# Layer 0 of a two-layer encoder: transposed inputs with the norm's factor applied behind the products, and the first output projection begun beside the last attention group

## The chip, the cores and the metric

The kernel runs on one core of one Trainium2 chip. The metric is the device time of one execution in microseconds (us). The kernel before was run three times: 2688.71, 2690.17 and 2694.2 us, median 2690.17 us.

Five engines work side by side, each with its own queue of instructions that it runs strictly in order: TensorE (PE, products into PSUM banks), VectorE (DVE), ScalarE (ACT), GpSimd (POOL), and SyncE (SP), which issues most DMA transfers. An instruction that waits holds up everything behind it on its engine. A PSUM bank holds 128x512 float32 numbers; there are eight.

## The reference, cut to what matters

```
h = x                                        # 1024 tokens, 1024 channels
mem_n = rmsnorm(mem, mem_norm_g)             # 256 memory tokens
for layer in range(2):
    u = rmsnorm(h, norm_g[layer, 0])
    mem_kv = mem_n @ w_mem_kv[layer]
    if layer == 0: y = mixer_window_attn(u, mem_kv, ...)   # this change is here
    else:          y = mixer_hgrn2(u, mem_kv, ...)
    h = h + rmsnorm(y, norm_g[layer, 1])
    h = h + rmsnorm(conv_ffn(rmsnorm(h, norm_g[layer, 2]), ...), norm_g[layer, 3])

rmsnorm(x, g) = x * rsqrt(mean(x*x, axis=-1) + 1e-6) * g
mixer_window_attn: q, k, v, xq = split(u @ w_in); rotary on q and k;
    16 heads of 64 over a band of 384 keys, 4 cross heads of 128 over mem_kv;
    y = concat(attention (1024 wide), cross (512 wide)) @ w_out
```

The factor `rsqrt(mean + 1e-6)` is one number for each token. It can be multiplied in before a product over the channels, or behind it.

## The kernel before, in words

Every float32 product is made of three products of a faster format: each operand is cut into a high and a low part (`split`: ACT rounds the high part, DVE subtracts for the low part), and `mm3` issues high x high, high x low and low x high. The normed input stands transposed in `uh` and `ul` (high and low; eight blocks of 128 channels by 1024 tokens). Weights come as units of 128x1024: `wunit` loads one into a staging buffer `st` (four of them), and cuts it into `wh`, `wl`, a ring of four.

**Start (`start`, `memory_kv`).** Rows of 128 tokens are loaded; `norm_T` (lines 105 to 121) squares and sums them on ACT (L100), raises the mean to the power -0.5 on POOL (L93, one number for each partition), multiplies on DVE (L112), turns them by eight transposes on PE (L116) and splits the result: first two tiles of memory rows into `mh`, `ml`, then eight tiles of `x` into `uh`, `ul`. `memory_kv` multiplies the memory by the key and value weights of both layers. For each of four heads it makes a 128x256 result of 24 matmuls in one of four banks `pb`, and ACT copies it out (L159), which frees the bank; then four units fill two banks of values at once, 48 matmuls of 512 columns, copied out at L172. Each unit is followed by a `step()`, which norms and turns one tile of `x`.

**Layer 0 (`window`).** `proj(g)` projects a group of four heads into two banks `pj`, multiplies by `cos` and `sin` (L274, L275), adds on POOL (L276, L277) and transposes into the bank `ptq`; `attend(g)` makes scores (L315, L316), softmax, transposes (L338) and `po` (L341, L342), and writes `o` to the HBM tensor `oT`. Cross-attention heads (`cross_unit`) stand between. Groups 0 to 2 alternate with projections; group 3 comes last, when `psq` (the three banks `pj`, `pj`, `ptq`) has been released.

**First output projection (`WOut`).** It has 12 blocks of 128 channels: 0 to 5 (heads of groups 0 to 2), 8 to 11 (cross heads), 6 and 7 (group 3). `open(3, 2)` takes the three released banks and, for five of the eight token tiles, multiplies the blocks 0 to 5 and 8 to 11 for the first half of the output columns beside `attend(3)`. Each call of `products` reads its blocks back from `oT` by a DMA (L436) and splits them again. `finish` adds the blocks 6 and 7, does the other three tiles, then the second half of the columns, and the norm. The class `Out`, which is in the kernel already, does the same for layer 1: it keeps blocks 0 to 7 in `uh`, `ul` themselves and multiplies from there:

```
def read(self, ks, c0, c1, eng):
    c = (slice(None), slice(ks[0], ks[-1] + 1), slice(c0, c1))
    raw = ul[c].bitcast(F32)
    eng.dma_start(raw, oT[self.l][ks[0]:ks[-1] + 1, :, c0:c1].rearrange("k p t -> p k t"))
    act.copy(uh[c], raw)
    dve.tensor_tensor(ul[c], raw, uh[c].bitcast(F32), op=ALU.subtract)
def begin(self, psb, tags, y0):       # for each tile t: read blocks 0 to 5, then
        ps = self.bank()
        self.kept(ps, t, self.groups[0], True, True)
        act.copy(y0[t], ps)
```

The order on each engine is not that of the code: a scheduler in the compiler sets it. `tc.high_priority` moves an instruction ahead of others that are ready.

Of the kernel before, what the change touches and what calls it, by code (L numbers as in the profile page):

```python
# [30 lines left out]
MEM_POOL = 1  # L31
# [15 lines left out]
def build(tc, A, out):  # L47
# [15 lines left out]
    nc.sync.dma_start(ident, A["ident"])  # L63
# [84 lines left out]
    def memory_kv(tp, psb, mh, ml, step):  # L148

        for l in range(2):  # L150
            km = tp.tile([P, 4, 256], F32, tag="km", bufs=1, name="km")
            vm = tp.tile([P, 2, 512], F32, tag="vm", bufs=1, name="vm")
            for h in range(4):
                wh, wl = wunit(A["wmk"][l, h], eng=pool if 4 * l + h < MEM_POOL else None)
                ps = psb.tile([P, 512], F32, tag="pb", name="pb")
                for k in range(KT):
                    c = slice(k * P, (k + 1) * P)
                    mm3(ps[:, :256], wh[:, c], wl[:, c], mh[:, k, :], ml[:, k, :], k == 0, k == KT - 1)
                act.copy(km[:, h, :], ps[:, :256])  # L159
                step()  # L160
# [10 lines left out]
            for t in range(2):  # L171
                act.copy(vm[:, t, :], pv[t])  # L172
# [12 lines left out]
    def cross_unit(l, h, b, head, wp, tags, w0, pair):  # L185
# [12 lines left out]
        for i in range(2):  # L198
# [6 lines left out]
            dve.tensor_scalar_mul(st["nm"][:, e], st["nm"][:, e], -XSCALE)  # L205
            for j in range(2):
                q = 2 * i + j
                act.activation(p[:, q, :], s[:, j, :], AF.Exp, bias=st["nm"][:, q:q + 1],
                               scale=XSCALE, accum_out=st["su"][:, q:q + 1])
# [17 lines left out]
    def window():  # L227
# [7 lines left out]
        nc.sync.dma_start(sin, A["sin"])  # L235
        wmask = ap_.tile([P, 384], F32, bufs=1, name="wmask")
# [15 lines left out]
        def proj(g):  # L252
# [6 lines left out]
            for b in range(2):  # L259
                rqs = []  # L260
                for tt in range(4):
# [17 lines left out]
                    act.copy(v[:, t, :64], ps[:, 320:])  # L279
                    dve.tensor_tensor(v[:, t, 64:], ps[:, 320:], v[:, t, :64].bitcast(F32), op=ALU.subtract)  # L280
# [19 lines left out]
        def attend(g, qkv):  # L300
            qs, kh, kl, v = qkv
            for b in range(2):
                for nn in range(4):
# [42 lines left out]
                    if nn % 2 == 1:  # L346
# [24 lines left out]
    class WOut:  # L371

        groups = (range(0, 6), range(8, 12), range(6, 8))

        def __init__(self, l, src, key, order):
            self.l, self.src, self.key, self.order = l, src, key, order
            self.pools = [[], [], []]
            self.pre, self.part, self.begun, self.us = {}, {}, {}, {}
            self.psb, self.tag, self.psb2 = None, "pb", None

        def open(self, npre, nsb):

            l = self.l
            self.w1 = tc.alloc_tile_pool(name=f"wa{l}", bufs=2, reuse_waits="tile")
            if self.psb is None:
                self.psb = tc.alloc_tile_pool(name=f"wopb{l}", bufs=npre, space=PSUM, reuse_waits="tile")
            self.pools = [[self.w1] for _ in range(3)]
            if l == 0:

                self.w1.tile([P, 512], F32, tag="part", bufs=nsb, name="part")  # L390
                for g in (0, 2):
                    self.operands(g)
                for _ in range(2):
                    for x in ("xwh", "xwl"):
                        self.w1.tile([P, 1024], F32R, tag=x, name=x)
                self.operands(1)
            self.load(0)
            for t in self.order[npre:npre + nsb]:
                ps = self.bank()
                self.products(ps, t, 0)  # L400
                self.products(ps, t, 1, True)
                self.part[t] = self.w1.tile([P, 512], F32, tag="part", bufs=nsb, name="part")
                act.copy(self.part[t], ps)
            for t in self.order[:npre]:
                self.pre[t] = self.bank()
                for g in range(2):
                    self.products(self.pre[t], t, g)

        def bank(self):
            if self.psb2:  # L410
                return self.psb2.tile([P, 512], F32, tag="pb2", name="pb")
            return self.psb.tile([P, 512], F32, tag=self.tag, name="pb")

        def load(self, b, n=6):
            for i, u in enumerate((0, 1, 2, 4, 5, 3)[:n]):
                if (b, u) not in self.us:
                    self.us[b, u] = wunit(A[self.key][b, u], pl=self.w1 if i >= RING else None)
            self.b = b

        def products(self, ps, t, g, last=False, first=False, left=False):  # L420

            ks = [k for k in self.groups[g] if not (left and k in self.begun[t])]
            n = len(ks)
            oh, ol, raw = (x[:, :n, :] for x in self.operands(g))
            self.rows_of(ps, t, ks, oh, ol, raw, g == 0 or first, g == 2 or last)

        def operands(self, g):
            pl = self.pools[g][0]
            self.pools[g] = self.pools[g][1:] + self.pools[g][:1]
            m = len(self.groups[g])  # L430
            return [pl.tile([P, m, P], dt, tag=f"{x}{g}", bufs=1, name=x) for x, dt in (("oh", F32R), ("ol", F32R), ("or", F32))]

        def rows_of(self, ps, t, ks, oh, ol, raw, first, last):
            n = len(ks)
            ts_ = slice(t * P, (t + 1) * P)
            self.read = nc.sync.dma_start(raw, oT[self.l][ks[0]:ks[0] + n, :, ts_].rearrange("k p t -> p k t"))  # L436
            split(oh, ol, raw)
            for i, k in enumerate(ks):
                wh, wl = self.us[self.b, k // 2]
                c = slice((k % 2) * 512, (k % 2 + 1) * 512)  # L440
                mm3(ps, oh[:, i, :], ol[:, i, :], wh[:, c], wl[:, c], first and i == 0, last and i == n - 1)

        def rows(self, wp, t):
            x = wp.tile([P, D], F32, tag="x", bufs=2, name="x")
            nc.sync.dma_start(x, self.src[t * P:(t + 1) * P, :])
            return x

        def finish(self):
            l = self.l
            self.wf = tc.alloc_tile_pool(name=f"wf{l}", bufs=1, side="right", reuse_waits="tile") if l == 0 else None  # L450
            wp = tc.alloc_tile_pool(name=f"wo{l}", bufs=2, side="right", reuse_waits="tile")
            psp = tc.alloc_tile_pool(name=f"wops{l}", bufs=2, space=PSUM, side="right", reuse_waits="tile")
            w2 = tc.alloc_tile_pool(name=f"wb{l}", bufs=2, reuse_waits="tile")
            self.psb2 = tc.alloc_tile_pool(name=f"wopc{l}", bufs=(3, 4)[l], space=PSUM, reuse_waits="tile")
            self.pools[0].append(w2)
            y0 = wp.tile([P, NT, 512], F32, bufs=1, name="y0")
            s0 = wp.tile([P, NT], F32, bufs=1, name="s0")
            for t in self.order:
                ps = self.pre.get(t) or self.bank()
# [40 lines left out]
            w2.release()  # L500
            self.w1.release()

# [978 lines left out]
```

## Time and profile before

| | |
|---|---|
| median of 3 runs | 2690.17 us |
| profiled execution, its own time | 2686.47 us |
| its span | 2684.7 us |
| mean granted TensorE clock | 0.993 |
| PE busy, share of span | 98% |
| first product on the memory | 13.99 us |
| first product of layer 0 (`pj`) | 67.77 us |
| first product of the feed-forward part | after 594.38 us |

Times in the profile count from the start of the span. A timeline row gives the start, the duration, the engine, the line, the operation, `out<-in`, the shape and, in brackets, how long the engine had been idle and what ended that. Durations of matmuls overlap: the rate is read from the starts of rows that follow each other. In a table by stretches the first number behind the stretch is its length, then the busy time of each engine, then the granted clock of PE, the share of the DMA engines and GB/s.

### The profile page before, as it was taken

What the parts mean: (1) busy time and instruction counts of PE and PEld (TensorE: products, weight loads), DVE (VectorE), ACT (ScalarE), POOL (GpSimd) and SP (SyncE); (2) the same over time, 40 slices, a digit from 0 to 9 for tenths busy, and PEclk for the clock granted to TensorE, in tenths of its full rate; (3) what the DMA queues carried; (4) which work ended last, traced back from release to release, by engine and by line L of the source; (5) the groups of instructions that cost most, each with busy time, mean ns of one, the idle gap of its engine ahead of it and who ended that gap; (6) DMA issues with size and microseconds to landing.
All of it is one profiled execution on the core that took longest, in us unless ns stands there. A gap on an engine that the chain in (4) does not pass through costs nothing.

```text
span 2684.7 us, 39333 instructions
## 1 busy us (share of the span) xinstructions
PE 2618.3 (98%) x14496; PEld 2200.0 (82%) x14496; DVE 1827.6 (68%) x3026; ACT 1384.6 (52%) x2530; POOL 469.4 (17%) x520
## 2 busy tenths in 40 slices
PE   8999999999999999999999999999999999999998
PEld 7888897788888887887888888888888788888886
DVE  6587787678656565478778686796757755656456
ACT  6367666645444445455455454545534444444453
POOL 1231110111111100032223132230211111110013
PEclk9999998999999999999999999999999999999999
DMA  7674213557877756674326252102436777774666
GB/s 281 213 166 104 60 28 117 176 183 181 216 199 200 205 165 243 191 241 157 103 84 177 76 120 70 48 29 83 150 119 178 183 202 210 198 205 160 220 196 228
DMA packets 204626, 427.00 MB, mean 159 GB/s; under 512 B 20112, under 2 KB 66576, under 8 KB 198800
## 3 DMA queue, kind: packets, MB, share of 16 engines
q1 hardware_dynamic: 171168, 326.68, 37.5%
q0 software_dynamic: 24544, 90.19, 16.1%
q10 hardware_dynamic: 8720, 7.60, 0.9%
q8 instruction: 114, 1.87, 0.3%
q14 instruction: 80, 0.66, 0.1%
HBM read 331.08 MB, written 117.44 MB: 167 GB/s over the span
## 4 chain that ended last, share of the span: by engine, by line
PE 77%; DVE 13%; ACT 4%; DMA 3%; issue 2%; POOL 1%; SPq 0%; DVEq 0%; ACTq 0%; POOLq 0%
PE X L638 27%; PE V L638 11%; PE pj L81 5%; PE pj L82 5%; PE Y L638 5%; PE pj L83 5%; PE pb L82 3%; PE pb L81 3%; PE pb L83 3%; DVE E L1194 1%; DVE ER L1229 1%; PE pt L338 1%; PE pt L116 1%; DVE wl L87 1%; PE po L1297 1%
## 5 line engine op out<-in xcount | busy, mean ns | idle before, releaser
L87 DVE TENSOR_TENSOR wl<-st,wh 128x1024 fp32r<-128x1024 f32 (+1 forms) x238 | 263.5, 1114 | 325.7 <-ACT wh L86 318.3
L86 ACT CAST wh<-st 128x1024 fp32r<-128x1024 f32 (+1 forms) x238 | 222.5, 937 | 295.2 <-PE X L638 196.2
L81 PE MATMUL pj<-uh,wh 128*128 128x512 f32 x512 | 204.1, 399 | 3.8 <-DVE xl L87 2.5
L638 PE MATMUL X<-wl,wh 128*128 128x512 f32 x528 | 204.8, 390 | 0.3 <-DVE wl L87 0.3
L638 PE MATMUL X<-wh,wl 128*128 128x512 f32 x528 | 204.6, 389 | 0.0
L82 PE MATMUL pj<-ul,wh 128*128 128x512 f32 x512 | 202.5, 396 | 0.1
L83 PE MATMUL pj<-uh,wl 128*128 128x512 f32 x512 | 201.6, 394 | 0.0
L638 PE MATMUL X<-wh 128*128 128x512 f32 x528 | 198.8, 390 | 1.7 <-DVE c L1014 0.9
L81 PE MATMUL pj<-wh,uh 128*128 128x384 f32 (+1 forms) x512 | 190.4, 372 | 4.2 <-DVE gs L1125 3.8
L82 PE MATMUL pj<-wl,uh 128*128 128x384 f32 (+1 forms) x512 | 187.3, 366 | 0.0
L83 PE MATMUL pj<-wh,ul 128*128 128x384 f32 (+1 forms) x512 | 186.8, 366 | 0.0
L77 DVE TENSOR_TENSOR wl<-st,wh 128x1024 fp32r<-128x1024 f32 (+1 forms) x92 | 119.9, 1310 | 28.1 <-ACT wh L76 27.4
L638 PE MATMUL V<-uh,wh 128*128 128x512 f32 x344 | 133.8, 389 | 0.0
L638 PE MATMUL V<-ul,wh 128*128 128x512 f32 x344 | 133.8, 389 | 0.0
L638 PE MATMUL V<-uh,wl 128*128 128x512 f32 x344 | 133.8, 389 | 0.0
L76 ACT CAST wh<-st 128x1024 fp32r<-128x1024 f32 (+1 forms) x99 | 99.9, 1015 | 50.5 <-PE pj L82 27.8
L638 PEld LDWEIGHTS X<-wh 128*128 128x128 f32 x528 | 99.1, 188 | 22.9 <-issue 1.3
L81 PEld LDWEIGHTS pj<-uh,wh 128*128 128x128 f32 x512 | 96.7, 189 | 24.2 <-DVE xl L87 2.9
L638 PEld LDWEIGHTS X<-wl,wh 128*128 128x128 f32 x528 | 99.1, 188 | 21.2 <-DVE wl L87 0.7
L638 PEld LDWEIGHTS X<-wh,wl 128*128 128x128 f32 x528 | 99.1, 188 | 20.8
L83 PEld LDWEIGHTS pj<-uh,wl 128*128 128x128 f32 x512 | 96.8, 189 | 19.2
L980 POOL TENSOR_TENSOR c<-c,g 128x512 f32<-128x512 f32 x24 | 43.4, 1828 | 393.8 <-PE X L638 162.8
(372 smaller groups left out, 7257.4 us busy)
## 6 DMA issues: line engine op xcount, KB each, us to landing
st<-hid SPq DMA_DIRECT2D x154, 256.0 KB, 3.1
st<-in_ffw_dram SPq DMA_DIRECT2D x108, 256.0 KB, 3.2
w2s<-in_ffw_dram POOLq DMA_DIRECT2D x24, 1024.0 KB, 7.9
st<-in_ffw_dram SPq DMA_DIRECT2D x46, 512.0 KB, 4.1
hid<-tt SPq DMA_DIRECT2D x88, 256.0 KB, 4.6
st<-w2s SPq DMA_DIRECT2D x88, 256.0 KB, 2.8
sx<-in_ffw_dram SPq DMA_DIRECT2D x84, 256.0 KB, 3.9
sy<-in_ffw_dram SPq DMA_DIRECT2D x42, 512.0 KB, 6.2
```

What stands on the lines that cost most here:

```text
L76: act.copy(h[:, :n], raw)
L77: (eng or dve).tensor_tensor(l[:, :n], raw, h[:, :n].bitcast(F32), op=ALU.subtract)
L81: pe.matmul(o, ah, bh, start=first, stop=False)
L82: pe.matmul(o, ah, bl, start=False, stop=False)
L83: pe.matmul(o, al, bh, start=False, stop=last)
L86: act.copy(h, src)
L87: dve.tensor_tensor(l, src, h.bitcast(F32), op=ALU.subtract)
L116: pe.transpose(ps[:, k, :], u[:, (4 * b + k) * P:(4 * b + k + 1) * P], ident)
L338: pe.transpose(tp[:, j, :], sm[:, j, c * P:(c + 1) * P], ident)
L638: pe.matmul(o, x, y, start=new, stop=e, skip_group_check=not first)
L980: pool.tensor_tensor(y[q][:, t, :], y[q][:, t, :], g3[:, c], op=ALU.mult)
L1194: dve.tensor_tensor_scan(B[:, rev], smask, a_[:, rev], 0.0, op0=ALU.mult, op1=ALU.add)
```

## The change

The host gives `x` and `mem` transposed as well (`xT`, `memT`) and the two gains as columns (`gT`). `start` no longer norms rows: it loads 128 channels at a time, and `scaled` makes the high and low parts of `x * g` directly (ACT, then DVE). The norm's factor is made apart. For the memory, ACT squares all of it, POOL folds eight blocks into one, PE sums over partitions by a product with ones (`pbc`, a copy of the 256 sums in every partition, and `pcc`), DVE adds epsilon, and POOL raises a whole 128x256 tile to the power -0.5 (`rsb`) and a 128x2 one (`rsm`). The keys are multiplied by `rsb` when they leave their banks (DVE; it was a copy on ACT), the values by `rsm`. For `x` the squares are added up on POOL in `acc`, and eight small products, one POOL power over 128x8 (`rs0`) and two DVE multiplications (`xsc`) follow `memory_kv`. `cos` and `sin` are multiplied by `rs0`, so are the values `v`, and the cross scores of layer 0 use `xsc` in place of a constant. The first memory unit is split on DVE like the others, no longer on POOL (`MEM_POOL` goes). No transposes are left in `start`: 80 matmuls of 128x128 are gone.

Layer 0's output projection uses `Out`. `psq` isn't released: `begin` multiplies blocks 0 to 5 of all eight tiles into its three banks and copies the results to `y0`. Group 3 writes `o` straight into blocks 6 and 7 of `ul` by DMA, not to `oT`.

```
-                wh, wl = wunit(A["wmk"][l, h], eng=pool if 4 * l + h < MEM_POOL else None)
+                wh, wl = wunit(A["wmk"][l, h])
...
-                act.copy(km[:, h, :], ps[:, :256])
+                if l == h == 0:
+                    begin()
+                dve.tensor_tensor(km[:, h, :], ps[:, :256], rsb, op=ALU.mult)
...
-                act.copy(vm[:, t, :], pv[t])
+                act.activation(vm[:, t, :], pv[t], AF.Copy, scale=rsm[:, t:t + 1])
...
+        dve.tensor_tensor(cos, cos, bc(rs0.unsqueeze(2), [P, NT, 32]), op=ALU.mult)
+        s2 = sin.rearrange("p t a b -> p t (a b)")
+        dve.tensor_tensor(s2, s2, bc(rs0.unsqueeze(2), [P, NT, 64]), op=ALU.mult)
...
-                    if nn % 2 == 1:
+                    if nn % 2 == 1 and g == 3:
+                        ts_ = slice((n - 1) * P, (n + 1) * P)
+                        oh, ol = uh[:, 6:8, ts_], ul[:, 6:8, ts_]
+                        for hp in range(2):
+                            nc.sync.dma_start(ul[hp * 64:(hp + 1) * 64, 6:8, ts_].bitcast(F32), o[:, hp::2, :])
+                        act.copy(oh, ol.bitcast(F32))
+                        dve.tensor_tensor(ol, ol.bitcast(F32), oh.bitcast(F32), op=ALU.subtract)
...
-        psq.release()
         ea.release()
         attend(3, cur)
-        wo0.open(3, 2)
+        wo0.open()
+        y0 = wo0.w1.tile([P, NT, 512], F32, bufs=1, name="y0")
+        wo0.begin(psq, ("pj", "pj", "ptq"), [y0[:, t, :] for t in range(NT)])
...
-            for t in self.order:
+            for i, t in enumerate(self.order):
+                if i == (6, 0)[l]:
+                    self.banks += late
+                    self.used = (3, 0)[l]
...
+        def scaled(h, l, raw, g):
+            act.activation(h, raw, AF.Identity, scale=g)
+            dve.scalar_tensor_tensor(l, raw, g, h.bitcast(F32), op0=ALU.mult, op1=ALU.subtract)
...
+        def memory_rstd():
+            for k in (0, 4):
+                act.activation(msq[:, k:k + 4], mT[:, k:k + 4], AF.Square)
+            for n in (4, 2, 1):
+                pool.tensor_tensor(msq[:, :n], msq[:, :n], msq[:, n:2 * n], op=ALU.add)
+            pb = pss.tile([P, 256], F32, name="pbc")
+            pe.matmul(pb, ones, msq[:, 0], start=True, stop=True)
+            ms = tp.tile([P, 256], F32, name="mms")
+            dve.tensor_scalar(ms, pb, 1.0 / D, EPS, op0=ALU.mult, op1=ALU.add)
+            with tc.high_priority(AHEAD):
+                pool.tensor_tensor(rsb, ms, bc(nhalf[:, 0:1], [P, 256]), op=ALU.pow)
...
+        left = [None, None] + list(range(KT))
...
+            raw = tp.tile([P, T], F32, tag="x", bufs=4, name="x")
+            nc.sync.dma_start(raw, A["xT"][k])
+            scaled(uh[:, k], ul[:, k], raw, gT[:, 1, k:k + 1])
...
+                sq = tp.tile([P, T], F32, tag="sq", bufs=2, name="sq")
+                act.activation(sq, raw, AF.Square)
+                pool.tensor_tensor(acc, acc, sq, op=ALU.add)
...
-    wo0 = WOut(0, A["x"], "wout0", list(range(NT)))
+    wo0 = Out(0, A["x"], "wout0", list(range(NT)))
```

What the scheduler makes of it is seen at three places. The first is POOL's queue at the start. Before, it holds the ten norm factors of one column each (`nrs`) and one split:

```order
L65 MEMSET nhalf 128x8
L93 ISA
L93 TENSOR_TENSOR nrs<-nms,nhalf 128x1 x2
L77 TENSOR_TENSOR wl<-st,wh 128x1024
L93 TENSOR_TENSOR nrs<-nms,nhalf 128x1 x8
```

Now it holds the folding of the memory's squares, two additions of `x` squares, the power over 256 columns (`rsb`), and the other additions behind it:

```order
L1277 TENSOR_TENSOR msq<-msq 128x1024
L1277 TENSOR_TENSOR msq<-msq 128x512
L1277 TENSOR_TENSOR msq<-msq 128x256
L1306 TENSOR_TENSOR acc<-acc,sq 128x1024 x2
L1283 TENSOR_TENSOR rsb<-mms,nhalf 128x256
L1289 TENSOR_TENSOR rsm<-mm_174,nhalf 128x2
L1306 TENSOR_TENSOR acc<-acc,sq 128x1024 x5
```

One power of 256 columns has taken the place of ten of one column.

The second is PE between the last key head and the first value unit of the first layer. Before, the products go on from heads to values with nothing between:

```order
L81 MATMUL pb<-mh,wh 128x256
L82 MATMUL pb<-ml,wh 128x256
L83 MATMUL pb<-mh,wl 128x256
L81 MATMUL pb<-wh,mh 128x512 x2
L82 MATMUL pb<-wl,mh 128x512
```

Now the sums over partitions stand inside the last head:

```order
L1279 MATMUL pbc<-msq,ones 128x256
L1286 MATMUL pcc<-ones,msq 128x1 x2
L80 MATMUL pb<-ml,wh 128x256
L81 MATMUL pb<-mh,wl 128x256
L79 MATMUL pb<-mh,wh 128x256
L80 MATMUL pb<-ml,wh 128x256
L81 MATMUL pb<-mh,wl 128x256
L79 MATMUL pb<-wh,mh 128x512
```

The 128x512 row is the first value product. It goes into the bank of head 0, and now waits for the DVE multiplication that reads `rsb` and empties that bank.

The third is PE at the beginning of `attend(3)` (`ps` are its scores, `pt` its transposes, `pb` the output projection). Before, the scores of four blocks of queries and the first `po` come before the first output product:

```order
L315 MATMUL ps<-kh,qs 128x384 x2
L342 MATMUL po<-pl,v 128x512
L338 MATMUL pt<-ident,sm 128x128 x4
L316 MATMUL ps<-kl,qs 128x384 x2
L81 MATMUL pb<-wh,oh 128x512
L82 MATMUL pb<-wl,oh 128x512
```

Now output products, 18 in a row for each tile, begin behind the first scores:

```order
L79 MATMUL po<-ph,kvh 128x512
L322 MATMUL ps<-kh,qs 128x256
L323 MATMUL ps<-kl,qs 128x256
L79 MATMUL pb<-wh,uh 128x512
L80 MATMUL pb<-wl,uh 128x512
L81 MATMUL pb<-wh,ul 128x512
```

The first two tiles' products, 36 matmuls, have moved ahead of nearly all scores of group 3.

More of the change, by code (lines that the diff above doesn't have):

```diff
@@ L29 @@
 STAGE = 4
-MEM_POOL = 1
 QKV_POOL = (0, 2, 2, 2)
@@ new lines, in start @@
+        mh = tp.tile([P, KT, 256], F32R, name="mh")
+        ml = tp.tile([P, KT, 256], F32R, name="ml")
+        for k in range(0, KT, 2):
+            act.dma_start(mT[:, k:k + 2], A["memT"][:, k:k + 2])
+        def scaled(h, l, raw, g):
+            act.activation(h, raw, AF.Identity, scale=g)
+            dve.scalar_tensor_tensor(l, raw, g, h.bitcast(F32), op0=ALU.mult, op1=ALU.subtract)
+        for k in range(KT):
+            scaled(mh[:, k], ml[:, k], mT[:, k], gT[:, 0, k:k + 1])
+        msq = tp.tile([P, KT, 256], F32, name="msq")
@@ new lines, in start @@
+        memory_kv(tp, psb, mh, ml, rsb, rsm, memory_rstd, step)
+        nc.sync.dma_start(ident, A["ident"])
+        pt = pss.tile([P, NT], F32, name="ptt")
+        for t in range(NT):
+            pe.matmul(pt[:, t:t + 1], acc[:, t * P:(t + 1) * P], ones[:, 0:1], start=True, stop=True)
+        ms = tp.tile([P, NT], F32, name="xms")
+        dve.tensor_scalar(ms, pt, 1.0 / D, EPS, op0=ALU.mult, op1=ALU.add)
+        pool.tensor_tensor(rs0, ms, nhalf, op=ALU.pow)
+        dve.tensor_scalar_mul(xsc[:, 0], rs0, XSCALE)
```

189 lines of the change are left out of this document (43 added, 146 removed).

## Prediction

> **What bounds the kernel now.** I read the page's first part, then tables by stretches for the two stages that the change touches, then their timeline rows.
>
> ```profile
> PE 2618.3 (98%) x14496; PEld 2200.0 (82%) x14496; DVE 1827.6 (68%) x3026; ACT 1384.6 (52%) x2530; POOL 469.4 (17%) x520
> ```
>
> PE is busy nearly always, so a change pays where PE idles, runs at a lower clock, or does work that can go. The table of the start and of the stretch from the last projection to the feed-forward part:
>
> ```profile
> 13.99:67.77 53.78, 53.63 (x354) 49.20 (x353) 42.26 (x51) 37.50 (x60) 6.20 (x8) 1.00 0.78 273
> 403.98:594.38 190.40, 180.17 (x839) 147.02 (x838) 136.11 (x278) 116.72 (x253) 21.18 (x24) 0.96 0.52 160
> 400.00:430.00 30.00, 24.80 (x99) 18.43 (x98) 27.13 (x69) 24.23 (x56) 4.10 (x4) 0.72 0.48 141
> 430.00:480.00 50.00, 50.00 (x254) 42.27 (x253) 33.40 (x90) 31.50 (x78) 0.00 (x0) 1.00 0.35 98
> 480.00:500.00 20.00, 15.96 (x79) 12.40 (x79) 11.18 (x21) 11.58 (x25) 0.00 (x0) 1.00 0.33 85
> ```
>
> At the start PE works without a pause from its first product on the memory (13.99 us) to the first product of layer 0 (67.77). POOL does 6 us in that time. The output stage loses 190.4 - 180.2 = 10.2 us to idle PE and 4% of the clock, 7.2 us: 17.4 us in all. Of it, 5.2 us idle and 28% of 30 us, 8.4, lie at 400 to 430, before the output products have begun, and 4.0 at 480 to 500, at the tail of `attend(3)`.
>
> The rates of PE come from starts of neighbouring rows: 0.21 us for a 256-column product just after PE has begun, 0.12 later, 0.227 for 512 columns, 0.17 for the 384 of a projection; four transposes take 0.44 us in the chain of waits.
>
> ```profile
> 15.10 0.41 PE L83 MATMUL pb<-mh,wl 128*128 128x256 f32 x1
> 15.31 0.41 PE L81 MATMUL pb<-mh,wh 128*128 128x256 f32 x1
> ...
> 21.15 0.28 PE L82 MATMUL pb<-ml,wh 128*128 128x256 f32 x1
> 21.27 0.28 PE L83 MATMUL pb<-mh,wl 128*128 128x256 f32 x1
> ...
> 61.65 0.39 PE L82 MATMUL pb<-wl,mh 128*128 128x512 f32 x1
> 61.87 0.39 PE L83 MATMUL pb<-wh,ml 128*128 128x512 f32 x1
> ...
> 67.77 0.33 PE L81 MATMUL pj<-wh,uh 128*128 128x384 f32 x1
> 67.94 0.34 PE L82 MATMUL pj<-wl,uh 128*128 128x384 f32 x1
> ```
> ```profile
> 17.80 0.44 PE pt L116 x4
> ```
>
> **The power over 256 columns.** The price that decides is one which the trace does not hold at this size. It holds the same POOL operation at one and at four columns (min/median/max in ns):
>
> ```profile
> L93 POOL TENSOR_TENSOR nrs<-nms,nhalf x34: 538/548/3790, 6.6 to 2043.7; 128x1 f32<-128x1 f32 x34
> L93 POOL TENSOR_TENSOR ors<-oms,nhalf x16: 1006/1036/1146, 1374.0 to 1937.9; 128x4 f32<-128x4 f32 x16
> ```
>
> Three more columns cost 488 ns, 0.163 us each. By that line 256 columns take 0.548 + 255 x 0.163 = 42.1 us (40.3 by the minima). The lower bound is POOL's additions:
>
> ```profile
> 80.08 0.86 POOL L276 TENSOR_TENSOR rq<-t,t 128x320 f32<-128x320 f32 x1 [0.30 <-DVE t L275]
> 80.92 0.31 POOL L277 TENSOR_TENSOR rq<-t,t 128x64 f32<-128x64 f32 x1
> ```
>
> 256 more columns cost 0.55 us there, 0.0021 us each, so at that rate the power takes 0.55 + 0.55 = 1.1 us. I take 42, because the rows of the power itself are nearer than those of another operation, and nothing in them shows columns that come for nothing.
>
> The Trainium skill, page "GPSIMD Engine Reference", section "3.1 Elementwise — side-by-side cycle accounting", counts about 2.6 cycles an element for a two-input elementwise instruction, some 2.2 ns at the page's 1.2 GHz. The additions agree with it; the power's 0.163 us a column does not, being 75 times that. An estimate by that page would be near 1 us, and the change then ends as in the first rival.
>
> **Who waits for it.** PE's order puts the first value product into the bank of head 0. Four banks hold the four heads, so PE can do 96 products (11.5 us warm) and must then wait until DVE has multiplied head 0 by `rsb`. DVE has put its multiplications behind all eight `ul` splits, which need no `rsb`.
>
> **When the power starts.** ACT has 21 instructions ahead of the square that POOL's second `acc` addition needs, and does that square too. The nearest rows:
>
> ```profile
> 1.18 0.42 SPq L1376 DMA_DIRECT2D x<-in_mem_dram  x1
> 5.08 1.06 ACT L100 ACTIVATE nu<-x 128x1024 f32<-128x1024 f32 x1 [3.06 <-DMA x<-in_mem_dram]
> 10.12 1.05 ACT L76 CAST wh<-st 128x1024 fp32r<-128x1024 f32 x1
> 11.24 2.53 POOL L77 TENSOR_TENSOR wl<-st,wh 128x1024 fp32r<-128x1024 f32 x1 [1.01 <-ACT wh L76]
> 19.71 0.38 ACT L159 COPY km<-pb 128x256 f32<-128x256 f32 x1
> ```
>
> Eight scalings of 128x256 at 0.38, two squares of 1024 columns at 1.06, four weight casts at 1.05, three scalings and three squares of `x` at 1.06: 3.0 + 2.1 + 4.2 + 6.4 = 15.7 us. The first 512 KB landed at 5.08; the first 256 KB of `memT` will be a little earlier, 4.5. So the square is done at 20.2. The two additions at 2.53 run from 18.1, when the first one's square is there, to about 23.2. `pbc` does not come later: the memory's squares end near 13, folding takes 2.5 + 1.3 + 0.7. I put the power at 23.5 to 65.6 us (by a slower DMA, 26).
>
> **The start, summed.** DVE's multiplication and two handovers take 0.7 us: PE resumes at 66.3. What is left for it: 48 x 0.227 + 96 x 0.12 + 48 x 0.227 = 33.3 us, the eleven small products at a transpose's 0.11 about 1, and a slow beginning as at 14 us, 16 products at 0.09 us extra, 1.5. `pj` begins at 102.1 in place of 67.77: **+34.3 us**. The removed transposes, 80 x 0.11 = 8.8 us, and PE's first product some 8 us earlier all lie before the end of the power and gain nothing. Queued behind the power on POOL are `rsm` (0.7) and five additions (12.7): three squares on ACT wait for those because `sq` has two buffers, and the next weight cast stands behind them, 10 us after the power; PE reaches it after 0.7 + 10.9 + 1.5, so it comes in time. SP's loads fill the four staging buffers meanwhile.
>
> **The beginning of layer 0.** Before, PE idles 2.1 + 0.45 us there, since `cos`, `sin` and the sink arrive late:
>
> ```profile
> 78.39 0.33 PE L286 MATMUL ptq<-ident,rq 128*128 128x128 f32 x1 [2.12 <-POOL rq L276]
> 79.17 0.66 PE L81 MATMUL pj<-wh,uh 128*128 128x384 f32 x1 [0.45 <-DVE v L280]
> ```
> ```profile
> 76.46 0.49 DVE L274 TENSOR_TENSOR t<-pj,cos 128x320 f32<-128x320 f32 x1
> ```
>
> They still come from the same place in SP's queue. DVE now has two more multiplications between their arrival and the first `t`, of 256 and 512 columns; at 0.49 for 320 they take 0.4 + 0.7: **+1.1 us**. The 128x8 power, 0.55 + 7 x 0.163 = 1.7 us, lies beside two tiles of projection (48 x 0.17 = 8.2 us). The scaled forms for `v` and the cross scores replace instructions of the same size, one for one: nothing.
>
> **The output stage.** All 576 products stay. Before, the first came at 426.95:
>
> ```profile
> 426.95 0.39 PE L81 MATMUL pb<-wh,oh 128*128 128x512 f32 x1
> ...
> 594.38 1.06 PE L116 MATMUL pt<-ident,nu 128*128 128x128 f32 x8 [0.99 <-DVE nu L112]
> ```
>
> Now 36 of them, 36 x 0.227 = 8.2 us, stand among the scores where 13.6 us were lost, and products of the second half of the columns stand ahead of the last `po`, where 4.0 us were idle. I take 8.2 + 4.0: **-12.2 us**. The bounds are -17.4, the whole loss, and 0: DVE is busy 27.1 of 30 us at 400 to 430, and if the scores wait for it just as long, the moved products only leave their old place empty. A new wait is possible: the `ul` reads of eight tiles stand in SP's queue between the writes of `o`, and PE waits for their splits with scores behind. They are issued while `proj(3)` still runs, so I charge nothing.
>
> **Sum.** 34.3 + 1.1 - 12.2 = +23.2 us. Against the profiled execution (2686.47, its span 2684.7 and 1.8 around it) 2709.7; the median of the runs shown is 3.7 above that execution, so I predict **2713 us**, 0.9% slower.
>
> **Rivals.** First, on the other side: the power is vectorised and takes what the additions take, 1.1 us. It ends at 24.6, PE resumes at 25.3, and with the same 35.8 us `pj` begins at 61.1, 6.7 earlier. Sum -6.7 + 1.1 - 12.2 = -17.8: 2672 us. For it: the 2.1 ns a column of the additions. Against it: 1 and 4 columns of the power. It decides if the power takes less than 42 - 23 = 19 us. The page on GpSimd named above would have it so. Second, a power that gets cheaper per column when there are many: at half the slope it takes 21 us, the start costs 34.3 - 21 = 13.3 and the whole 2.2: 2692; at three quarters, 32 us and 2703. Nothing in the rows speaks for it but that they stop at four columns. Third, the output stage gives nothing and DVE, which works on two inputs all through the power, stretches it as the slowest one-column row (3.8 in place of 0.55 us) shows can happen: 46 us and no gain, 34.3 + 4 + 1.1 = +39: 2730. That the early products do not fill PE's gaps is part of it.
>
> **Chances.** Forecast 0.66, first rival 0.14, second 0.10, third 0.10. A difference under 0.2% (5 us) cannot be told from none here. The first rival is faster but for its edge; half the second is within 0.2% or just above; the rest is slower: faster 0.15, same 0.05, slower 0.80. The forecast alone spans 2703 to 2724 (power 40 to 44 us, start 23 to 26, output -17 to -3); 2690 to 2731 takes in the second and third rival and leaves out the first.
>
> **What would show it.** A POOL row of about 42 us for `rsb` at L1283; PE idle from about 20 to 66 us until the DVE row at L159; `pj` near 102. First `pb` output product near 405 plus 35, no idle stretch around the last `po`. The forecast falls if the `rsb` row is under 20 us, or if PE does not wait for it.

## Result, and the profile after

The changed kernel takes 2716.68 us (median of 4 runs, 2713.09 to 2721.6), the kernel before 2690.73 us beside it (4 runs). The ratio is 1.0097, with a 95% interval of 1.0079 to 1.0114: 26 us slower. The forecast was 2713 us. The profiled execution took 2714.96 us, its span is 2713.2. One execution in this document, of `e2_64_columns`, ran at a granted clock of 0.75 and took 3264.14 us; the median of that kernel is over the nine others.

First, from the page, the busy times of the engines, the clock row of the slices, and the lines of the chain that ended last:

```profile
PE 2609.4 (96%) x14438; PEld 2193.3 (81%) x14438; DVE 1822.4 (67%) x3004; ACT 1379.8 (51%) x2488; POOL 536.5 (20%) x523
...
PEclk6999999999999999999999999999999999999999
...
PE X L515 30%; PE V L515 11%; PE pj L79 6%; PE pj L80 6%; PE pj L81 5%; PE Y L515 5%; PE pb L79 4%; PE pb L80 4%; PE pb L81 4%; POOL rsb L1283 2%; DVE E L1071 1%; PE pt L345 1%; DVE ER L1106 1%; PE po L1174 1%; PE pt L114 1%
```

PE does 9 us less work than before and the kernel is longer. The clock row has one weak slice, the first. One instruction of POOL, `rsb`, holds 2% of the chain. Its row in POOL's timeline (start, duration, and in brackets the idle time ahead of it), with all else that POOL does from 13 to 110 us:

```profile
13.82 6.58 POOL L1277 TENSOR_TENSOR msq<-msq 128x1024 f32<-128x1024 f32 x3 [12.84 <-ACT msq L1275]
20.36 6.66 POOL L1306 TENSOR_TENSOR acc<-acc,sq 128x1024 f32<-128x1024 f32 x2
26.98 42.13 POOL L1283 TENSOR_TENSOR rsb<-mms,nhalf 128x256 f32<-128x256 f32 x1
69.10 0.70 POOL L1289 TENSOR_TENSOR rsm<-mm,nhalf 128x2 f32<-128x2 f32 x1
69.77 13.12 POOL L1306 TENSOR_TENSOR acc<-acc,sq 128x1024 f32<-128x1024 f32 x5
108.46 1.65 POOL L1315 TENSOR_TENSOR rs<-xms,nhalf 128x8 f32<-128x8 f32 x1 [25.57 <-DVE xms L1314]
```

And PE behind it, at the end of its wait and at the first product of layer 0:

```profile
69.72 0.76 PE L79 MATMUL pb<-wh,mh 128*128 128x512 f32 x1 [46.10 <-DVE km L159]
70.28 0.63 PE L80 MATMUL pb<-wl,mh 128*128 128x512 f32 x1
70.70 0.63 PE L81 MATMUL pb<-wh,ml 128*128 128x512 f32 x1
...
83.11 0.28 PE L79 MATMUL pb<-mh,wh 128*128 128x256 f32 x1
...
94.51 0.39 PE L79 MATMUL pb<-wh,mh 128*128 128x512 f32 x1
...
105.70 1.84 PE L1312 MATMUL ptt<-ones,acc 128*128 128x1 f32 x16
107.41 0.43 PE L79 MATMUL pj<-wh,uh 128*128 128x384 f32 x1
```

PE stands still for 46.1 us until the DVE row at L159 empties the first bank, and that row waits for the power.

To compare kernels I cut each span at three places: the first `pj`, the last `pj` of the projections of layer 0, and the last transpose of the output stage's norm. The table of stretches (length, then busy time of PE, PEld, DVE, ACT, POOL, then PE's clock, DMA share, GB/s) of before:

```profile
0.00:67.77 67.77, 57.39 (x369) 52.34 (x369) 46.49 (x58) 44.74 (x71) 10.34 (x16) 1.00 0.78 281
67.77:403.80 336.03, 321.75 (x1834) 289.69 (x1833) 245.58 (x668) 208.69 (x540) 67.46 (x92) 0.98 0.43 114
403.80:606.50 202.70, 192.47 (x902) 157.26 (x901) 141.09 (x286) 119.30 (x259) 23.07 (x28) 0.96 0.53 161
606.50:2684.70 2078.20, 2046.64 (x11398) 1700.67 (x11395) 1394.42 (x2016) 1011.84 (x1663) 368.54 (x386) 1.00 0.56 162
```

and of the changed kernel:

```profile
0.00:107.41 107.41, 52.79 (x311) 47.18 (x311) 47.94 (x46) 44.80 (x51) 68.97 (x18) 0.78 0.49 170
107.41:438.50 331.09, 319.32 (x1822) 287.94 (x1822) 250.09 (x672) 215.52 (x540) 69.24 (x91) 0.98 0.46 121
438.50:636.00 197.50, 191.21 (x914) 156.90 (x913) 131.14 (x272) 107.47 (x236) 29.26 (x30) 0.98 0.40 127
636.00:2713.20 2077.20, 2046.11 (x11398) 1701.23 (x11396) 1393.18 (x2016) 1011.98 (x1663) 369.06 (x386) 1.00 0.57 162
```

The start costs 39.6 us more, the attention 4.9 less, the output stage 5.2 less, and the rest is the same within 1 us.

### The profile page after: what moved, and what is told of

It reads as the page before. It is cut to its first block, busy times and chain, and to the rows that moved or that the text cites. A ratio compares the mean times of both kernels' runs of the same rounds, so it can differ in the third digit from the quotient of the medians.

```text
span 2713.2 us, 39049 instructions
## 1 busy us (share of the span) xinstructions
PE 2609.4 (96%) x14438; PEld 2193.3 (81%) x14438; DVE 1822.4 (67%) x3004; ACT 1379.8 (51%) x2488; POOL 536.5 (20%) x523
## 4 chain that ended last, share of the span: by engine, by line
PE 82%; DVE 10%; POOL 3%; ACT 2%; DMA 1%; issue 1%; DVEq 0%; SPq 0%; ACTq 0%; POOLq 0%
PE X L515 30%; PE V L515 11%; PE pj L79 6%; PE pj L80 6%; PE pj L81 5%; PE Y L515 5%; PE pb L79 4%; PE pb L80 4%; PE pb L81 4%; POOL rsb L1283 2%; DVE E L1071 1%; PE pt L345 1%; DVE ER L1106 1%; PE po L1174 1%; PE pt L114 1%
```

## The experiments

Theory: the power over 256 columns holds four banks, PE waits for one of them, and nothing else makes the kernel slower; the output half of the change gains about 12 us. Rivals: the start is bound by what stands beside or behind the power (ACT, DVE, POOL's additions); or the output half gains nothing and the shorter stretch has another cause.

This is the table of the stages, read from each run's trace as above (us), with the medians of the runs (attention: from the first to the last `pj`; output stage: from there to the last transpose of its norm):

| kernel | start | attention | output stage | the two together | rest | time |
|---|---|---|---|---|---|---|
| before | 67.8 | 336.0 | 202.7 | 538.7 | 2078.2 | 2690.7 |
| changed | 107.4 | 331.1 | 197.5 | 528.6 | 2077.2 | 2716.7 |
| e1_small_power | 77.1 | 328.5 | 197.8 | 526.3 | 2076.6 | 2685.0 |
| e2_64_columns | 75.9 | 329.3 | 196.3 | 525.6 | 2083.2 | 2683.8 |
| e3_six_banks | 95.2 | 330.0 | 198.6 | 528.6 | 2080.0 | 2703.1 |
| e4_start_alone | 107.9 | 325.5 | 207.4 | 532.9 | 2081.4 | 2724.1 |
| e5_output_alone | 68.1 | 337.3 | 192.9 | 530.2 | 2079.8 | 2678.8 |
| e6_adds_on_dve | 72.5 | 335.6 | 193.8 | 529.4 | 2085.4 | 2686.9 |
| e7_adds_on_dve_six_banks | 64.0 | 329.6 | 196.2 | 525.8 | 2079.1 | 2670.6 |
| e8_long_power_adds_on_dve | 107.3 | 336.0 | 190.0 | 526.0 | 2083.5 | 2716.8 |
| e9_ident_in_begin | 66.5 | 334.3 | 193.8 | 528.1 | 2082.1 | 2678.0 |
| e10_ident_by_act | 64.3 | 332.0 | 200.0 | 532.0 | 2082.9 | 2678.8 |
| e11_start_repaired_alone | 64.5 | 325.5 | 206.5 | 532.0 | 2088.7 | 2676.8 |

The column "rest" is code that no edit touches. It spreads over 12 us between profiled executions: e11's is the longest of its five runs, 2687.02 us against a median of 2676.78, and e6, e7 and e9, in which PE's order is the same there row for row, have 2085.4, 2079.1 and 2082.1. So the readings go by the other columns and by the medians, and what lies under some 5 us between two kernels is left open. The other columns spread too: the changed kernel, e1, e2, e3 and e7 have one and the same order of PE through the whole attention, and they differ by 2.6 us there and by 3.0 in the two stages together.

### The power made small

```
+        nc.sync.dma_start(ident, A["ident"])
...
-                pool.tensor_tensor(rsb, ms, bc(nhalf[:, 0:1], [P, 256]), op=ALU.pow)
...
+                pool.tensor_tensor(rsm, ms2, nhalf[:, :2], op=ALU.pow)
...
+                for t in range(2):
+                    dve.tensor_scalar_mul(diag[:, t], ident, rsm[:, t:t + 1])
...
+                pe.matmul(pb, ones, diag.rearrange("p t c -> p (t c)"), start=True, stop=True)
+                dve.tensor_copy(rsb, pb)
...
-        nc.sync.dma_start(ident, A["ident"])
```

The identity `ident` is needed earlier now, so its load moves from behind `memory_kv` to the head of the start.

> The root is raised for two columns only (rsm, 128x2, 0.70 us in the changed kernel), and TensorE spreads it over the 256 columns: ident times rsm on VectorE, one product with ones, one copy. Theory (the 42-us power alone holds the four banks): POOL still has the folds and two additions of acc ahead, so rsm starts near 27 as the long power did; with 0.7 for the power, 1 for the diagonal and 1 for product, copy and multiplication PE resumes near 31 in place of 69.7, and pj starts near 68 in place of 107.4. Time 2716.7 - 39 = 2677, which is 0.5% below the kernel before. Rival A (behind the power stands as much work of ACT, DVE and POOL, seven additions of 3.3 us, which then becomes the bound of the start): PE waits again behind the head products, pj at 80 to 90, time 2690 to 2700. Rival B (the wait is not the power's): under 5 us gained, above 2710.

Measured: 2685.0 us (ratio to before 0.9980, 0.9970 to 0.9989), 31.7 us below the changed kernel. `pj` starts at 77.1. So the power was the wait: 30 of the 39.6 us are gone with it. But 9 us are missing against the theory. DVE and POOL show where, in this run's timelines:

```profile
28.41 1.21 DVE L75 TENSOR_TENSOR wl<-st,wh 128x1024 fp32r<-128x1024 f32 x1
29.55 2.56 DVE L1288 TENSOR_SCALAR diag<-ident,rsm 128x128 f32<-128x128 f32 x2
32.03 3.38 DVE L75 TENSOR_TENSOR wl<-st,wh 128x1024 fp32r<-128x1024 f32 x1
35.33 0.41 DVE L1291 COPY rsb<-pbc 128x256 f32<-128x256 f32 x1
35.66 3.03 DVE L75 TENSOR_TENSOR wl<-st,wh 128x1024 fp32r<-128x1024 f32 x1
```
```profile
27.38 1.69 POOL L1285 TENSOR_TENSOR rsm<-mm,nhalf 128x2 f32<-128x2 f32 x1 [1.23 <-DVE mm L1283]
29.04 15.20 POOL L1308 TENSOR_TENSOR acc<-acc,sq 128x1024 f32<-128x1024 f32 x5
```

The split of a weight takes 1.21 us while POOL is not adding and 3.38 while it is; POOL's additions take 3.0 each, where its one split of the same size took 2.53 in the kernel before. The chain from `rsm` to the multiplication passes through both. This is a part of rival A: not the amount of work behind the power, but that two engines hold each other up.

### A quarter of the columns

```
-                pool.tensor_tensor(rsb, ms, bc(nhalf[:, 0:1], [P, 256]), op=ALU.pow)
+                pool.tensor_tensor(rsb, ms[:, :64], bc(nhalf[:, 0:1], [P, 64]), op=ALU.pow)
```

> The power is raised for the first 64 of the 256 columns only and these 64 are used for all (the other 192 tokens of the memory get wrong scales: a part of the computation is left out). Theory (a price per column, 0.548 + 63 x 0.163): the rsb row takes 10.8 us in place of 42.1, PE resumes near 38.4, pj starts near 76, time 2716.7 - 31 = 2685. Rival A (a price per instruction for long rows, not per column): the rsb row stays above 20 us and the time above 2694. Rival B (the columns are cheap and something else made the row long): under 3 us, and the time as in e1.

Measured: 2683.8 us. POOL's row:

```profile
26.87 11.53 POOL L1284 TENSOR_TENSOR rsb<-mms,nhalf 128x64 f32<-128x64 f32 x1
```

11.53 us for 64 columns and 42.13 for 256: 0.159 us for each of the 192 columns between. The price goes by the column to the end. The 64 columns took a little more than the 10.8 of the theory (0.174 us for each behind the first). And `pj` at 75.9 is where the theory put it. One PE wait of 15.4 us is left at the same row L159.

### Two more banks

```
-        psb = tc.alloc_tile_pool(name="mpb", bufs=4, space=PSUM, reuse_waits="tile")
+        psb = tc.alloc_tile_pool(name="mpb", bufs=6, space=PSUM, reuse_waits="tile")
```

(`pcc` and `ptt` then share a bank.)

> The power stays at 42 us, but the products of the start have six banks in place of four, so PE can do the 48 value products of the first layer (48 x 0.227 = 10.9 us) before it needs a bank that waits for rsb. Theory (PE waits for a free bank, and for nothing else): the wait shrinks from 46 to about 35 us, pj starts near 97, time 2716.7 - 11 = 2706. Rival A (ACT and DVE stand behind the power too, with squares that wait for POOL's additions and with the next weights behind those): PE waits for weights after the power, gain under 3 us, above 2713.

Measured: 2703.1 us (ratio 1.0045, 1.0028 to 1.0061), 13.5 below the changed kernel, `pj` at 95.2. The power's row is still 42.13 us. PE's waits, in us in total, times, longest:

```profile
PE pb L79 <- DVE km L159: 26.6, 1, 26.6
...
PE pb L80 <- DVE wl L75: 5.6, 1, 5.6
```

46.1 has become 26.6 for the bank, and 5.6 for a split that DVE does beside POOL's additions. That the wait for the bank fell by 19.5 and not by the 11 of the theory has this reason: those 5.6 us, and slow products behind them (every 0.43 us until 34, at a granted clock of 0.50), fill a part of the time that PE would else have waited. It is a wait for a bank. Rival A is out as the bound of the start: its wait for weights is there, but it costs nothing while the power still runs.

### Each half of the change alone

The start alone: the changed kernel with `WOut` for layer 0 and its reads as before.

```
-    wo0 = Out(0, A["x"], "wout0", list(range(NT)))
+    wo0 = WOut(0, A["x"], "wout0", list(range(NT)))
```

> The transposed inputs with the root behind the products, and the output projection of layer 0 as it was before. Theory (all of the loss is the start's; the two parts add): the start costs 39.6 us more than before, layer 0's beginning about 0, and the output stage gains nothing: time 2690.7 + 39 = 2730. Rival A (the shorter stretch from pj to the feed-forward part, 10.9 us, comes from the start's change, by the changed scale of the cross scores or the order that the scheduler makes): time near 2717, as with both parts. Rival B (the parts hinder each other): above 2736.

Measured: 2724.1 us (ratio 1.0129, 1.0114 to 1.0145): 33.4 above before, 7.4 above both halves together. The start costs the same 40 us. That the loss is less than 39 comes in the main from the attention, which is 10.5 us shorter than before, while the output stage is 4.7 longer. So 5.8 us of the shorter stretch belong to the first half of the change, which nothing in the prediction had. PE's order from the first `pj` on differs there from before's at the 22nd row, though the code of the attention issues the same products.

The output half alone: before, with `wo0 = Out(...)`, `psq` kept, and the `o` of group 3 written straight into `ul`.

> The start of before, and the output projection of layer 0 begun beside the last attention as in the changed kernel. Theory 1 (the prediction's term: early products fill PE's idle and slow stretch around the last attention): -12.2 us, 2690.6 - 12 = 2678. Theory 2 (the parts add, and part of the 10.9 us belongs to the start's change: the run of the start alone came out 33.4 slower, 7.4 above the changed kernel): -7 us, 2683. Rival (the moved products only leave their old place empty): within 2 us of 2690.6.

Measured: 2678.8 us (5 runs; ratio 0.9949, 0.9936 to 0.9963), 12.2 below the 2691.0 of before beside it. Theory 1 gave 12.2. PE's order is before's for the first 1270 of the some 1520 rows up to the last `pj`, and the attention takes 337.3 us, as before's 336.0. The gain is in the output stage, and there it lies where the prediction looked for it. Before, the stretch behind the last `pj`:

```profile
403.80:440.00 36.20, 31.00 (x125) 23.36 (x125) 30.74 (x85) 27.24 (x68) 1.15 (x3) 0.76 0.47 145
```

and with the output half:

```profile
405.40:440.00 34.60, 31.56 (x148) 25.33 (x148) 28.97 (x76) 24.84 (x58) 3.54 (x4) 0.95 0.49 153
405.40:598.30 192.90, 188.38 (x914) 156.50 (x914) 130.75 (x273) 106.82 (x236) 28.77 (x29) 0.99 0.41 133
```

PE does 148 products there in place of 125, the clock is 0.95 in place of 0.76, and idle PE in the whole stage falls from 10.2 to 4.5 us. The tail has its part in this: behind 490 us idle PE falls from 4.2 to 1.5.

### The additions on VectorE

The kernel of e1 with

```
-                pool.tensor_tensor(msq[:, :n], msq[:, :n], msq[:, n:2 * n], op=ALU.add)
+                dve.tensor_tensor(msq[:, :n], msq[:, :n], msq[:, n:2 * n], op=ALU.add)
...
-                pool.tensor_tensor(acc, acc, sq, op=ALU.add)
+                dve.tensor_tensor(acc, acc, sq, op=ALU.add)
```

> As e1_small_power, and the additions of squares (three folds, seven of acc) on VectorE in place of POOL. Theory (in e1 POOL's additions and VectorE's work on two inputs held each other up: splits of 2.7 to 3.4 us in place of 1.22, additions of 3.3): all splits take 1.2 us again and the ten additions cost VectorE 10.7 us more; the multiplication by rsb still stands late in VectorE's order, behind five splits and four additions after the diagonal, so PE resumes near 36 and pj starts near 72 in place of 77.1; time 2685 - 5 = 2680. Rival A (the splits were long for another reason, such as the loads): they stay above 2 us, pj above 80, time 2690 or more. Rival B (VectorE becomes the bound): pj near 80, 2688.

Measured: 2686.9 us (10 runs), so above the 2680. The start did what was expected: every split takes 1.21 to 1.28 us, an addition 1.22, and `pj` starts at 72.5. But the 4.6 us gained there do not reach the end: attention and output stage take 529.4 us in place of e1's 526.3, with another order of PE that the scheduler made from the 19th row behind the first `pj` on, and the rest is longer, for which no cause was found. So contention made the splits long, which e6 was to tell; the forecast of its time failed. With six banks as in e3:

> As e6_adds_on_dve, with six banks for the start's products. Theory (what is left of PE's wait in e6 is a wait for banks, which e3 shortened): PE goes on with the value products of layer 0 as their weights come, no wait above 5 us is left, pj starts near 64; time 2685 - 13 = 2672, 0.7% below the kernel before. Rival (VectorE or ACT is the bound of the start, so banks change nothing): pj as in e6, 2680.

Measured: 2670.6 us (2668.74 to 2670.76; ratio 0.9919, 0.9906 to 0.9933), 0.8% below the kernel before and 1.7% below the changed one. Its first two stretches, and PE's longest waits in the first 110 us:

```profile
0.00:64.00 64.00, 50.86 (x310) 44.94 (x311) 48.75 (x59) 44.03 (x51) 2.04 (x8) 1.00 0.84 290
64.00:393.60 329.60, 319.26 (x1820) 288.25 (x1821) 248.75 (x670) 215.45 (x540) 69.18 (x91) 0.98 0.45 121
```
```profile
PE pb L79 <- ACT wh L74: 9.0, 1, 9.0
PE ptq L293 <- DVE kl L85: 2.3, 1, 2.3
PE pb L80 <- DVE wl L75: 1.7, 1, 1.7
```

No wait for a bank is left, and the clock column shows 1.00 for the start, which is 3.8 us shorter than before. (The column misses the slow beginning that all these kernels have: up to 13.2 us products of 256 columns come every 0.21 us here, behind that every 0.12.) The transposed inputs pay once the power is small, the additions are off POOL and two more banks are given.

### The long power without POOL's additions

The changed kernel with the edit of e6 alone.

> The changed kernel with its long power left at 256 columns, and the ten additions of squares on VectorE in place of POOL. Theory (the power began 3.5 us later than forecast because POOL's folds and two additions stood ahead of it and ran slowly beside VectorE): rsb starts near 22.5 (in e6 the short power started at 22.64) in place of 26.98, still takes 42.1, ends near 64.7; PE resumes near 65.3 and pj starts near 102.5, as the prediction had it. Time 2716.7 - 4.5 = 2712, if the rest of layer 0 takes what it took; the scheduler gives it another order from the 13th row behind the first pj on, and e6, with another order too, took 6 us more there, so up to 2718. Rival (the power waits for something else, or stretches): rsb starts after 25 or takes over 43 us.

Measured: 2716.8 us, no gain. Half of the theory held:

```profile
23.80 46.65 POOL L1283 TENSOR_TENSOR rsb<-mms,nhalf 128x256 f32<-128x256 f32 x1 [22.82 <-DVE mm L1288]
```

The power starts at 23.8, which is where the prediction had it (23.5), so POOL's own folds and additions made it late. But it takes 46.65 us. DVE works beside it without a pause until 40.5 us, so for 16.7 us; in the changed kernel it did so until 37.9, for 10.9 us, and the power took 42.13. What starts 3.2 us earlier lasts 4.5 longer. The amount of DVE's work alone does not explain it: in e3 DVE is busy for 15.6 us inside the power, 13 of them without a pause, and the power takes 42.13. In e8 five of DVE's instructions inside it are additions, in e3 none. No run separates these, so what stretched the power stays open. The attention has an order of its own here too.

### The order behind the start

Two more places for the load of `ident` in e7's kernel, behind the first weights on SP, and on ACT's queue:

> As e7_adds_on_dve_six_banks, with the load of ident issued by SP behind the first weights and not ahead of them. Theory (in e7 the load stands ahead of the first weights, and PE's first product waits 9.0 us for them, in the changed kernel 7.6): PE begins at 7.6, pj starts near 62.5, time 2670.6 - 1.5 = 2669. PE's order in layer 0 differs from e7's from the 49th row on. Rival (that order, or one like it, costs what e6's cost): 2675.

> As e7_adds_on_dve_six_banks, with ident loaded on ACT's queue. The start is the same but for 1.5 us at its beginning; PE's order in layer 0 parts from e7's and from the changed kernel's at the 19th row, as e6's did, and follows e6's for 27 rows. Theory (what e6 lost is its other order of layer 0: 335.6 us from the first to the last pj in place of 329.6 in e7): the attention takes 335 us again and the time is 2674 to 2678. Rival (e6's loss was chance): 329 us and 2669.

Measured: 2678.0 and 2678.8 us, both about 8 slower than e7, where e9's theory wanted 1.5 less. e9 begins its first product at 7.6 us as expected, and `pj` still comes later, at 66.5: among others, PE waits a second time for weights, 0.9 us, and 1.6 for the diagonal. Attention and output stage take 2.3 us more than in e7, which is within the spread of kernels with the same order. In e10 `pj` starts at 64.3, as in e7, and these two stages take 532.0 us in place of 525.8. The theory of e10 said 335 us for the attention alone; it is 332.0, and 3.8 of the loss stand in the output stage. So a start of the same length with another order behind it goes with some 6 us more here, as a sum of both stages, and not in the place that e6 pointed to.

The last run is the first half of the change with its start repaired as in e7, and the output projection of before:

> The start of e7_adds_on_dve_six_banks with the output projection of layer 0 as before: the transposed inputs, root behind the products, without their long power, and nothing else. PE's order in layer 0 is that of e4_start_alone for 1606 rows. Theory (the start's loss was all due to the power, and the parts nearly add): pj at 64 in place of 67.8 before, 3.8 us, and the shorter attention that e4 showed, 5.8 us with the output stage: 2690.6 - 9.6 = 2681. The output part then brings the further 10 us to e7's 2670.6. Rival (the shorter attention belongs to e4's long pause, not to its order): only the start's 3.8 us are left, 2687.

Measured: 2676.8 us (5 runs; ratio 0.9952, 0.9939 to 0.9966), 14 below before, 4 better than expected. The attention takes 325.5 us as in e4, now without the long pause ahead of it, and with the output stage 532.0, before 538.7. So the pause is not what makes it shorter, and the rival is out. What e4 and e11 have in common is PE's order, the same for 1606 rows; the changed kernel, e1, e2, e3 and e7 share it for 1249 rows, which is most of the attention, and take 328.5 to 331.1 there. Before and e5, with the other order, take 336.0 and 337.3. No run changed that order and nothing else, so that the order makes the difference is argued and not shown. Between e11 and e7 the output half alone differs: it takes 10.3 us off the output stage, puts 4.1 onto the attention, and is worth 6.2 by the medians.

## Why the prediction was right

It said 2713 us, 0.9% slower; 2716.7 was measured. By its own steps:

- **The power.** 42.1 us from the rows of one and four columns; 42.13 measured. Had it gone by POOL's additions, as the first rival did (1.1 us), the sign would have been wrong. The Trainium skill, page "GPSIMD Engine Reference", section "3.1 Elementwise — side-by-side cycle accounting", gives that lower price for elementwise work; no run agrees with it for a power. The second rival, cheaper columns when there are many, fell with e2's 0.159 us. That the kind of price was right is no luck; that the size came out to 0.1 us in part is: the same line gives 10.8 us for e2's 64 columns, where 11.53 was measured, and the same power took 46.65 in e8.
- **Who waits.** PE waits 46.1 us for the bank of head 0, as forecast; e3 shows that it is the bank.
- **When the power starts.** 23.5 forecast, 26.98 measured: the mis-sized term of the start. ACT was in time (the square of the second addition ended at 20.7; forecast 20.2; the sum counts 20 instructions with that square, as the trace has them, and not the 21 ahead of it that the prediction names). POOL was slow: the folds took 6.58 us in place of 4.5, the two additions 6.66 in place of 5.1. The prediction had POOL's rate from a row of before beside which DVE worked mostly on a PSUM bank (`pt`), and did not ask what DVE's splits with both inputs in SBUF do to it. e6 and e8 show the start at 22.6 and 23.8 without that work on POOL.
- **From the wait to `pj`.** 35.8 forecast, 37.7 measured. The first 48 value products took 13.4 us (83.11 - 69.72) in place of 10.9 + 1.5: after the pause a product of 512 columns comes every 0.43 us for 4 us, not 0.227. The next heads took 11.4, the next values 11.2. The eight small sums before `pj` took 1.7 where 1 was charged for all eleven.
- **The beginning of layer 0.** +1.1 forecast. PE's idle time there is 1.6 us (1.09 + 0.51) in place of 2.6, so it came out about -1: DVE waits for `sk` behind its first use of `pj` now, and before it did so ahead of it.
- **The output stage.** -12.2 forecast, by 8.2 around the scores and 4.0 at the tail. Alone (e5) it is 12.2 by the medians and 9.8 in the stage's rows: 5.7 less idle time, 4.1 less busy time at the higher clock. In the changed kernel the stage shows only 5.2, and 4.9 in the attention. With the order that the first half brings, the output half takes 9.9 us off the stage (207.4 in e4, 197.5) and puts 5.6 onto the attention (325.5, 331.1). So the two halves do not add: beside the first one, it is worth 7.4 us by the medians (e4). The signs that the prediction named are there: the first output product comes at 444.9 us, 337.5 behind the first `pj`, where 359.2 lay between them before, and products into `po` wait 0.5 us in place of 4.1.
- **The sum.** The start was forecast 5.3 us too small. Attention and output stage together gave -10.1, and were forecast at 1.1 - 12.2 = -11.1, but not by the forecast's reasons alone: e4 has -5.8 of it without the output half, by an order that was not in the sum, and this stands where part of the output half's gain was lost. That the two come within 1 us of each other is luck. With -1.0 in the rest, the span grew by 28.5 us in place of 23.2; the medians, by 26. The forecast's own range of 2703 to 2724 is not the sum of its bounds, which gives 2706 to 2727; 2716.7 lies in both.
- **The third rival.** Its stretched power (46 us) did not occur in the changed kernel, but it can occur: 46.65 in e8, with another mix of DVE's work beside it.

## What to carry to other kernels

Price an operation by the rows of that same operation, at whatever sizes the trace has them: its slope per column told more than any other instruction on that engine. When a root is needed along the free axis, take it for one column per 128 tokens and let TensorE spread it (a diagonal and a product with ones, here 1.5 to 3.9 us of POOL in place of 42). And before work goes to an idle POOL, see what DVE does at that time: in the start of e1, with the ten additions on POOL, DVE is busy for 54.8 us; in that of e6, where it does the additions itself, for 48.7.

## What the runs showed of the hardware

- A power on POOL takes 0.70 us for 2 columns, 1.65 for 8, 11.53 for 64 and 42.13 for 256: from size to size, each further column costs 0.16 to 0.18 us.
- POOL's additions and DVE's work on two inputs hold each other up: a DVE split of 1024 columns takes 1.21 us alone and up to 3.38 beside them, an addition on POOL about 3.3 in place of 2.53. The power is different. While it ran for 42 us, DVE did its splits at nearly full speed:

```profile
28.03 3.90 DVE L75 TENSOR_TENSOR wl<-st,wh 128x1024 fp32r<-128x1024 f32 x3
31.86 1.27 DVE L1264 SCALAR_TENSOR_TENSOR ul<-x,gT,uh 128x1024 fp32r<-128x1024 f32 x1
33.05 1.21 DVE L75 TENSOR_TENSOR wl<-st,wh 128x1024 fp32r<-128x1024 f32 x1
34.19 3.66 DVE L1264 SCALAR_TENSOR_TENSOR ul<-x,gT,uh 128x1024 fp32r<-128x1024 f32 x3
```

  These are rows of the changed kernel, inside the power's 26.98 to 69.11: eight splits, 1.2 to 1.3 us each on the mean. The Trainium skill, page "SBUF — State Buffer", section "SBUF: two separate sides", says that the port which the two engines share is locked for a whole instruction and that the other engine fully blocks. The additions fit that (3.38 is about 1.2 and most of an addition); the power does not, as DVE would then have stood still until 69 us. Where one of the two gives way, it is the power: 46.65 us in e8, and `rsm` 1.54 to 3.88 us in e6, e7, e9 and e10 in place of 0.70. But it does not always: in e3 it took 42.13 us beside 15.6 us of DVE's work.
- After 46 us without products PE's granted clock is 0.50 for 4 us (69.7 to 74.0), and products of 512 columns come every 0.43 us in that time in place of 0.23. In e3 a pause of 5.6 us was enough for the same (0.50 from 29.6 to 34.0).
- A change at the start changed the scheduler's order of PE in the attention behind it, where nothing was edited, and kernels with the same output half but another order differ there by up to 9 us (328.5 to 337.3), of which the output stage gives back a part (525.6 to 532.0 for both); kernels with the same order differ by 2.6 us there. That the order is the cause is argued, not shown. With such a scheduler, a difference of a few us between two kernels is not yet the price of the edit.
